# Swapping the two engines that issue loads and stores in a transfer-bound channel shuffle

## The chip, the cores and the metric

The kernel runs on one core of one Trainium2 chip. SyncE, ScalarE and VectorE are three of its engines, each with its own list of instructions. An engine that issues a transfer only hands it over (0.3 to 0.6 us in these traces); the core's 16 DMA engines then move the bytes, and the transfer has landed when all of them have arrived. The metric is the device time of one execution in microseconds (us), lower is better; a profile is a separate look at one execution, whose span is about 1.8 us shorter than its timed value. A run that is more than 1.5% above the fastest run of its own kernel counts as slow and is left out of ratios; where that happened it is said.

## The reference

A channel shuffle in float32: within every pixel, 256 channels seen as 8 groups of 32 are transposed to 32 by 8. No value changes.

```python
batch, h, w, c = 16, 64, 64, 256          # groups = 8
x = x.reshape(batch, h, w, groups, c // groups)
x = x.transpose(0, 1, 2, 4, 3)
return x.reshape(batch, h, w, c)
```

That is 67.11 MB in and 67.11 MB out.

## The kernel before

The pixels are cut into 16 tiles. `_SIZES` counts pixels per partition, so a tile of 38 is 128 rows of 38 x 256 floats = 38,912 contiguous bytes each, both in memory and on chip. Three input buffers, two output buffers. One engine, SyncE, issues all loads; VectorE transposes with one strided copy per tile; ScalarE issues all stores and does nothing else.

```python
_SIZES = [4, 8, 16] + [38] * 12 + [28]
_IN_BUFS = 3
_OUT_BUFS = 2
...
    for q in _SIZES:
        in_tile = in_pool.tile([P, biggest * c], F32, name="in_tile")
        nc.sync.dma_start(out=in_tile[:, : q * c], in_=rows(x_flat, first, q))      # line 47
        out_tile = out_pool.tile([P, biggest * c], F32, name="out_tile")
        nc.vector.tensor_copy(                                                      # line 49
            out=out_tile[:, : q * c].rearrange("p (i j g) -> p i j g", j=CPG, g=G),
            in_=in_tile[:, : q * c].rearrange("p (i g j) -> p i j g", g=G, j=CPG),
        )
        nc.scalar.dma_start(out=rows(out_flat, first, q), in_=out_tile[:, : q * c])  # line 53
        first += P * q
```

## Time and profile before

| | before |
|---|---|
| time, median of 3 | 316.71 us (316.44 to 317.62) |
| span of the profile | 314.7 us |
| VectorE busy | 119.2 us, 38% |
| share of the 16 DMA engines taken by the two queues | 49.8% + 49.4% |
| rate in the steady part | 433 GB/s |

The prediction below shows the lines behind this table. One more view of the kernel before is needed later: the timeline of the copies (start, duration, operation; in brackets the idle time of VectorE before it and what ended it).

```profile
20.36 3.90 DVE L49 COPY out_tile<-in_tile 128x4096 f32<-128x4096 f32 x1 [11.75 <-DMA out_dram<-out_tile]
34.50 8.75 DVE L49 COPY out_tile<-in_tile 128x9728 f32<-128x9728 f32 x1 [10.24 <-DMA out_dram<-out_tile]
51.03 8.75 DVE L49 COPY out_tile<-in_tile 128x9728 f32<-128x9728 f32 x1 [7.78 <-DMA out_dram<-out_tile]
74.00 8.80 DVE L49 COPY out_tile<-in_tile 128x9728 f32<-128x9728 f32 x1 [14.22 <-DMA out_dram<-out_tile]
```

Each of these copies waits for the store two tiles earlier, so their distances are the times of single stores: 14.1, 16.5 and 23.0 us, for stores whose rows have 8, 16 and 38 KB. Each store gives 128/16 = 8 rows to each DMA engine. At 433/16 = 27 GB/s per engine a row takes 0.30, 0.61 and 1.44 us. If every store row must let one 38 KB load row (1.44 us) go first, 8 turns make 8 x (1.44 + 0.30) = 13.9, 8 x (1.44 + 0.61) = 16.4 and 8 x (1.44 + 1.44) = 23.0 us. All three fit: an engine takes turns between the two queues by rows, and the length of a row does not count.

The distances alone would also fit turns of several rows at a time. The page's list of queues (packets, MB, share of the 16 engines; q1 carries the loads, q10 the stores), asked for 109.15 to 110.58 us and for 110.58 to 112.01 us, settles that:

```profile
q10 hardware_dynamic: 13, 0.51, 81.8%
q1 hardware_dynamic: 3, 0.12, 18.9%
...
q1 hardware_dynamic: 13, 0.51, 81.8%
q10 hardware_dynamic: 3, 0.12, 18.9%
```

In the time of one row, 13 store rows and 3 load rows start on the 16 engines; in the next it is the other way round, and so on in the two windows after these. An engine takes one row from each queue in turn.

### The profile page before, as it was taken

The numbers are of one execution on the slowest core, as the hardware profiler recorded it, in microseconds if no ns is written. First come the engines' busy times: TensorE is split into PE (matmuls) and PEld (weight loads), VectorE is DVE, ScalarE is ACT, GpSimd is POOL, SyncE is SP. The second block draws the span as 40 slices with busy tenths as digits, with TensorE's granted clock in tenths as the row PEclk, the third lists the DMA queues.
The fourth block names the chain that finished last, engine by engine and source line by source line (L and its number), as shares of the span: only waits on it lengthen the run. The fifth ranks groups of instructions, "written<-read, shape, count | busy, mean of one in ns | idle before, by whom it ended". The sixth has DMA issues, their size and how long they took to land.

```text
span 314.7 us, 133 instructions
## 1 busy us (share of the span) xinstructions
DVE 119.2 (38%) x16; POOL 0.2 (0%) x4
## 2 busy tenths in 40 slices
DVE  3040645505506407407308209109109019046620
POOL 0000000000000000000000000000000000000000
DMA  8999999999999999999999999999999999999997
GB/s 308 452 398 454 413 419 466 396 475 396 455 415 445 425 430 440 425 445 415 455 396 470 401 465 406 460 411 460 411 460 411 460 411 455 428 395 454 455 418 306
DMA packets 4608, 134.22 MB, mean 427 GB/s; under 512 B 512, under 2 KB 512, under 8 KB 768
## 3 DMA queue, kind: packets, MB, share of 16 engines
q1 hardware_dynamic: 2304, 67.11, 49.8%
q10 hardware_dynamic: 2304, 67.11, 49.4%
HBM read 67.11 MB, written 67.11 MB: 427 GB/s over the span
## 4 chain that ended last, share of the span: by engine, by line
DMA 75%; DVE 20%; issue 0%; SPq 0%; DVEq 0%
DMA out_dram<-out_tile 74%; DVE out_tile L49 20%; DMA in_tile<-in_x_dram 2%; SPq L47 0%; DVEq L49 0%
## 5 line engine op out<-in xcount | busy, mean ns | idle before, releaser
L49 DVE COPY out_tile<-in_tile 128x9728 f32<-128x9728 f32 (+4 forms) x16 | 119.2, 7449 | 181.4 <-DMA out_dram<-out_tile 175.9
L71 POOL MEMSET const-bfloat16-1.0<- 128x1 bf16 x1 | 0.1, 102 | 0.0
L71 POOL MEMSET const-uint8-127<- 128x1 uint8 x1 | 0.1, 102 | 0.0
L71 POOL MEMSET const-float32-1.0<- 128x1 f32 x1 | 0.1, 99 | 0.0
L71 POOL MEMSET const-float32-0.0<- 128x1 f32 x1 | 0.1, 98 | 0.2 <-issue 0.2
## 6 DMA issues: line engine op xcount, KB each, us to landing
in_tile<-in_x_dram SPq DMA_DIRECT2D x12, 4864.0 KB, 46.8
out_dram<-out_tile ACTq DMA_DIRECT2D x12, 4864.0 KB, 37.0
in_tile<-in_x_dram SPq DMA_DIRECT2D x1, 3584.0 KB, 43.8
out_dram<-out_tile ACTq DMA_DIRECT2D x1, 3584.0 KB, 13.3
in_tile<-in_x_dram SPq DMA_DIRECT2D x1, 2048.0 KB, 11.0
out_dram<-out_tile ACTq DMA_DIRECT2D x1, 2048.0 KB, 26.7
in_tile<-in_x_dram SPq DMA_DIRECT2D x1, 1024.0 KB, 5.4
out_dram<-out_tile ACTq DMA_DIRECT2D x1, 1024.0 KB, 25.8
```

What stands on the lines that cost most here:

```text
L49: nc.vector.tensor_copy(out=out_tile[:, : q * c].rearrange("p (i j g) -> p i j g", j=CPG, g=G), in_=in_tile[:, : q * c].rearrange("p (i g ...
L71: nc = _bacc.Bacc("TRN2", target_bir_lowering=False, num_devices=1)
```

## The change

The intent is to see whether it matters which engine issues which direction: the loads move to ScalarE and the stores to SyncE. Nothing else changes; the waits and the order of each list are the same.

```diff
-        nc.sync.dma_start(out=in_tile[:, : q * c], in_=rows(x_flat, first, q))
+        nc.scalar.dma_start(out=in_tile[:, : q * c], in_=rows(x_flat, first, q))
...
-        nc.scalar.dma_start(out=rows(out_flat, first, q), in_=out_tile[:, : q * c])
+        nc.sync.dma_start(out=rows(out_flat, first, q), in_=out_tile[:, : q * c])
```

## The prediction

> **What bounds the kernel now.** I read the page of the profile first: the busy table, the 40 slices and the queues.
>
> ```profile
> DVE 119.2 (38%) x16; POOL 0.2 (0%) x4
> ...
> DMA  8999999999999999999999999999999999999997
> GB/s 308 452 398 454 413 419 466 396 475 396 455 415 445 425 430 440 425 445 415 455 396 470 401 465 406 460 411 460 411 460 411 460 411 455 428 395 454 455 418 306
> ...
> q1 hardware_dynamic: 2304, 67.11, 49.8%
> q10 hardware_dynamic: 2304, 67.11, 49.4%
> HBM read 67.11 MB, written 67.11 MB: 427 GB/s over the span
> ```
>
> The only compute engine, VectorE, is busy 38% of the span. The 16 DMA engines are busy in every slice, with only the first and last below nine tenths. The two queues carry the same bytes and packets and fill 49.8% + 49.4% = 99.2% of what 16 engines have. So the transfers are the bound, and the GB/s row only wobbles because a slice catches more or fewer packet ends.
>
> Next I cut the span at the period of the copies (23 us, from the starts of the copies in the timeline) and at its two ends. The columns are the stretch, its length, VectorE and GpSimd busy time, clock, share of the DMA engines and GB/s.
>
> ```profile
> 152.00:175.00 23.00, 8.79 (x2) 0.00 (x0) 1.00 1.00 433
> 175.00:198.00 23.00, 8.85 (x2) 0.00 (x0) 1.00 1.00 433
> ...
> 1.50:1.70 0.20, 0.00 (x0) 0.00 (x0) 1.00 0.00 0
> 1.70:2.00 0.30, 0.00 (x0) 0.00 (x0) 1.00 1.13 205
> ...
> 312.00:313.00 1.00, 0.00 (x0) 0.00 (x0) 1.00 0.53 229
> 313.00:313.50 0.50, 0.00 (x0) 0.00 (x0) 1.00 0.01 0
> ```
>
> In the steady state the engines are full at 433 GB/s. Nothing moves before 1.7 us or after about 313 us. The ledger of the span is therefore: 134.22 MB / 433 GB/s = 310.0 us of transfer at full rate, 1.7 us of head, 1.7 us of tail (314.7 - 313.0), and 314.7 - 310.0 - 3.4 = 1.3 us of lost transfer while filling and draining. The timed run of the profiled execution is 316.46 us for a span of 314.7, so 1.8 us lies outside the span.
>
> Last come the waits, with engine, line, releaser, total us, times and longest.
>
> ```profile
> DVE out_tile L49 <- DMA out_dram<-out_tile: 175.9, 14, 14.6
> DVE out_tile L49 <- DMA in_tile<-in_x_dram: 5.5, 2, 4.1
> ...
> SPq L47 <- DVE out_tile L49: 224.4, 13, 22.2
> ```
>
> VectorE waits for an output buffer to be stored, 14 times; it waits for input only for the first two tiles. SyncE waits for a copy to free an input buffer. These waits say that everything stands behind the full transfer engines; none of them leaves an engine empty.
>
> **What the Trainium skill says.** "DMA: Bandwidth & Descriptors", section "Issuing engines are not separate DMA queues", says that DMAs from the scalar, sync or GpSimd engine all run on the same 16 DMA engines and interleave, so that the issuer only matters for the time of issuing. The trace agrees as far as it can: the two queues' shares add up to the one pool of 16. The same page, "SWDGE vs HWDGE vs iDMA", says a DMA issued from ACT is of the hardware kind just as one from SP; both queues are listed above as hardware_dynamic with 2304 packets each. The same page, "Queues, rings and completion order", says that each DMA engine goes round-robin between the queue rows, a whole packet at a time. That can be tested, because the first stores are small and meet large loads:
>
> ```profile
> in_tile<-in_x_dram SPq DMA_DIRECT2D x12, 4864.0 KB, 46.8
> out_dram<-out_tile ACTq DMA_DIRECT2D x12, 4864.0 KB, 37.0
> ...
> in_tile<-in_x_dram SPq DMA_DIRECT2D x1, 512.0 KB, 3.3
> out_dram<-out_tile ACTq DMA_DIRECT2D x1, 512.0 KB, 15.1
> ```
>
> The 512 KB store has 128 rows of 4 KB, 8 on each engine (128/16). One engine moves 433/16 = 27 GB/s, so a 4 KB packet is 0.15 us and a 38 KB row of a large load (9728 floats, 38912 bytes) is 1.44 us. If each store packet waits for one load packet, the store takes 8 x (1.44 + 0.15) = 12.7 us plus some 2 us of latency, that is 14.7; shown is 15.1. So the turns go one for one, and with equal packets each queue has half. "Perfetto Trace Analysis", section "Roofline", puts the ceiling of a single core at its 16 DMA engines, about 435 GB/s; 433 in the stretches above agrees, and leaves no room for a faster kernel with the same bytes.
>
> **The change part by part.** Nothing is added or removed. The two compiled programs compared instruction by instruction are equal on VectorE, GpSimd and TensorE; on ScalarE and SyncE the 16 loads and 16 stores change places, in the same order, with the same shapes and the same waits. Buffers stay at three and two. The cost is thus only in issuing:
>
> - First load, on the path: nothing can move before it. SyncE issues it at 0.73 us; its later load issues have a median of 328 ns, ScalarE's of 362 ns. So plus 0.03 us, perhaps a little more if ScalarE leaves the start barrier later.
> - The 15 other loads: 15 x 0.034 = 0.5 us in all, but each load is issued about a whole tile before it is needed. A load is issued when the copy three tiles earlier ends; its own copy starts 3 x 23 - 8.8 = 60 us later, and it lands after 46.8 us, so 13 us are spare. Hidden, 0.
> - The 16 stores: each gets about 0.03 us shorter on SyncE, and the engines have the rest of another transfer to move meanwhile. The last store is issued at 300.6 us, while the one before it, issued at 288.1, is still in flight. Hidden, 0.
> - The end: SyncE waits for the last stores at line 85 whichever engine issued them; issuing the stores first delays it by nothing, as its list is then empty. 0.
> - The sum is +0.03 us of 316.7, a hundredth of a per cent, below the spread of the three runs (316.44 to 317.62).
>
> **The rivals.**
>
> First, the turns might not be fair: one row (q1 or q10) may be favoured, and the swap would give the favour to the other direction. For it speaks only that the two directions have different landing times, 46.8 against 37.0 us; but that difference comes from how many transfers are queued behind one another, and the 15.1 us above says one for one. If stores were favoured, loads would come later, and the 13 us spare (6 us for the last load: VectorE is still waiting 5.95 us for a store before the last copy) would take it. Only a shift beyond that empties the engines; a period could then lose at most a few us, some 1% to 3%.
>
> Second, issuing on ScalarE could be a serial bottleneck: a load's issue and its semaphore waits sit on one in-order queue. Against it: one load per 23 us at 0.36 us of issue. Even 1 us of delay per load would be hidden by the 13 us. Worth at most 0.3 us, at the start.
>
> Third, a gain: SyncE's shorter issue for the stores, which are what VectorE waits for, could shorten the 175.9 us of waits. But these waits are transfer time of full engines; 0.03 us earlier into a queue with work before it changes nothing. A gain of 2% would need a span of some 308.4 us, or 305.0 without head and tail: 134.22 MB / 305.0 us = 440 GB/s, above any long stretch of the trace.
>
> **Range and chances.** 316.7 us, the median before plus 0.03. The range is the spread of the runs before, opened by about 0.4 us downwards for another draw and kept above: 316.0 to 317.6. Two per cent either way is 6.3 us; faster is excluded by the rate, slower needs the unfair turns. So 0.01, 0.98, 0.01.
>
> **What would show it right or wrong.** Right: 433 GB/s and a share of 1.00 in the 23 us stretches, the queues' shares swapped but adding to 99%, VectorE waiting some 176 us for stores, first bytes at about 1.75 us, the 512 KB store again near 15 us. Wrong: a head longer by over 0.3 us (ScalarE starts late); a stretch with a DMA share below 0.95, or VectorE waiting for loads in mid-kernel (unfair turns); landings of the 512 KB store much off 15 us.

## The result, and the profile after

The changed kernel takes 316.47 us (median of 6 runs, 316.39 to 317.35), the kernel before in the same rounds 316.63 us (316.44 to 317.62). The ratio is 0.9994 with a 95% interval of 0.9977 to 1.0012: the same. Ratios here are the mean time of one kernel's fast runs over the mean of the other's in the same rounds, so they are not quite the ratio of the medians.

From the page after its two queues (packets, MB, share), and then from the list of waits the largest (engine, line, what it waited for, total us, times, longest):

```profile
q10 hardware_dynamic: 2304, 67.11, 50.0%
q1 hardware_dynamic: 2304, 67.11, 49.3%
```

```profile
DVE out_tile L49 <- DMA out_dram<-out_tile: 176.2, 14, 15.0
```

The two queues have changed places in the list and are still full together (99.3%). VectorE waits for stores 176.2 us where it waited 175.9. The issue table after (operation, count, KB each, median us to landing) for the large tiles:

```profile
in_tile<-in_x_dram ACTq DMA_DIRECT2D x12, 4864.0 KB, 47.1
out_dram<-out_tile SPq DMA_DIRECT2D x12, 4864.0 KB, 37.0
```

Landing times stayed with the direction (46.8 and 37.0 before) and did not follow the engine. The first copy starts at 4.11 us, before at 4.09.

The profiled execution after happens to be its slowest run: a span of 315.6 us against 314.7. Two stretches of it (columns as in the prediction):

```profile
175.00:198.00 23.00, 8.84 (x2) 0.00 (x0) 1.00 1.00 433
...
221.00:244.00 23.00, 8.20 (x2) 0.00 (x0) 1.00 0.98 418
```

In the second stretch a pair of copies (212.50 and 236.07 us) is 23.57 us apart instead of 22.97; an earlier pair (50.88 and 74.64 us) lost 0.8 us. These are single hiccups of the transfers. Four of the six runs after have 316.4 to 316.5 us and so none of that size, and the kernel before has runs of 317.2 and 317.6, so they say nothing about the change.

### The profile page after: what moved, and what is told of

Its sections match the earlier page's. It is cut to its first block, busy times and chain, and to the rows that moved or that the text cites. A ratio compares the mean times of both kernels' runs of the same rounds, so it can differ in the third digit from the quotient of the medians.

```text
span 315.6 us, 133 instructions
## 1 busy us (share of the span) xinstructions
DVE 119.8 (38%) x16; POOL 0.2 (0%) x4
## 3 DMA queue, kind: packets, MB, share of 16 engines
q10 hardware_dynamic: 2304, 67.11, 50.0%
q1 hardware_dynamic: 2304, 67.11, 49.3%
## 4 chain that ended last, share of the span: by engine, by line
DMA 75%; DVE 20%; issue 0%; ACTq 0%; DVEq 0%
DMA out_dram<-out_tile 74%; DVE out_tile L49 20%; DMA in_tile<-in_x_dram 2%; ACTq L47 0%; DVEq L49 0%
## 5 line engine op out<-in xcount | busy, mean ns | idle before, releaser
L49 DVE COPY out_tile<-in_tile 128x9728 f32<-128x9728 f32 (+4 forms) x16 | 119.8, 7489 | 181.6 <-DMA out_dram<-out_tile 176.2
## 6 DMA issues: line engine op xcount, KB each, us to landing
in_tile<-in_x_dram ACTq DMA_DIRECT2D x12, 4864.0 KB, 47.1
```

The costliest lines, as they stand in the source:

```text
L49: nc.vector.tensor_copy(out=out_tile[:, : q * c].rearrange("p (i j g) -> p i j g", j=CPG, g=G), in_=in_tile[:, : q * c].rearrange("p (i g ...
```

## The experiments

The theory: 16 full DMA engines set the time, and the issuing engine, SyncE or ScalarE, matters neither for the issue cost (hidden) nor for the share of the engines (turns are per row). The rivals of the prediction were unfair turns, a slower issuer that delays loads, and earlier stores that help. A delay can be made large enough to see, and turns can be made unequal on purpose.

### Loads issued late (e3, e9)

The changed kernel, with eight ScalarE copies into the buffer ahead of a load:

```diff
+        if i >= 5:                       # e9: if 8 <= i < 15
+            for k in range(8):
+                nc.scalar.copy(out=in_tile[:, :2400], in_=scratch[:, :])
         nc.scalar.dma_start(out=in_tile[:, : q * c], in_=rows(x_flat, first, q))
```

> The changed kernel, with eight ScalarE copies of 2400 columns into the input tile ahead of every load from the sixth on: each of these loads is issued some 17 us later (an estimate), far more than the 0.03 us by which the two engines differ. Theory: a load's 47 us to landing are mostly time behind the load before it, so a load issued 17 us later lands in about 30 us; nothing waits; 316.3 to 317.8 us, VectorE waits for loads in mid-kernel under 3 us in total. Rival (the spare is only the 13 us between landing and use, as the prediction has it): 4 us per round of three buffers, 3 P = 17.5 + 47 + 8.8, so P = 24.4 instead of 23 us, times 11 tiles: about 331 us, with VectorE waiting for loads.

Measured: 320.88 us (319.30 to 322.15; ratio 1.0132). Neither number: far from the rival's 331, but not the same either. The windows of the profile (stretch, length, VectorE, ScalarE, GpSimd busy, clock, DMA share, GB/s) show where:

```profile
35.00:60.00 25.00, 18.32 (x2) 24.22 (x12) 0.00 (x0) 1.00 0.92 376
...
129.00:152.00 23.00, 9.19 (x1) 17.61 (x9) 0.00 (x0) 1.00 1.00 433
```

From 35 to 60 us the engines were partly empty: the first large tiles come only 14 and 16.5 us apart, ScalarE needs 17.6 us per delayed load, and it fell behind (busy 24.22 of 25 us). In the steady part the engines are full at 433 GB/s despite the delay. So the delay was moved to the steady part alone:

> As the late loads before, but the delay of some 17.5 us stands only ahead of seven loads in the steady part (the ninth to the fifteenth tile), so that ScalarE has no backlog from the early tiles, which come 14 and 16.5 us apart. Theory: a late load is hidden in the steady part: 316.3 to 317.8 us, and the loads it concerns land about 17 us sooner after issue. Rival (the 1.3 per cent of the earlier run came from the late issue itself): 318.5 us or more.

Measured: 317.01 us against 316.78, ratio 1.0003 (0.9986 to 1.0020). The issue table of this run:

```profile
in_tile<-in_x_dram ACTq DMA_DIRECT2D x12, 4864.0 KB, 28.5
```

The load is issued some 17.6 us later and lands 18.6 us sooner after issue than the 47.1 us of the changed kernel. Most of a load's landing time is time behind the load before it. A delay some 500 times the 0.034 us by which the two issuers differ is hidden in the steady part.

### Stores issued late (e5)

The kernel before, with two in-place ScalarE copies ahead of ten stores:

```diff
+        if 5 <= i < 15:
+            for k in range(2):
+                nc.scalar.copy(out=out_tile[:, :2400], in_=out_tile[:, :2400])
         nc.scalar.dma_start(out=rows(out_flat, first, q), in_=out_tile[:, : q * c])
```

> The kernel before (stores on ScalarE), with two ScalarE copies in place on 2400 columns of the output tile ahead of ten of the stores: each of these is issued some 4.4 us later (an estimate). Theory: a store issued that much later still finds the store before it in flight (it has 14 us to go), so it lands in about 33 us instead of 37; the time stays: 316.3 to 317.8 us. Rival (VectorE waits 176 us for stores, so when a store is issued sets the pace): 2 P = 8.8 + 4.4 + 37, P = 25.1 instead of 23 us, times 10: about 337 us.

Measured: 317.19 us against 316.52, ratio 1.0015 (0.9999 to 1.0031): the same.

```profile
out_dram<-out_tile ACTq DMA_DIRECT2D x12, 4864.0 KB, 32.5
```

The stores land 4.5 us sooner after issue (32.5 for 37.0): the delay of 4.38 us is paid out of the time in the queue. VectorE's 176 us of waiting for stores is waiting for full engines; when a store is issued does not set its length, within these 4.4 us.

### A late first load (e4)

```diff
+        if i == 0:
+            for k in range(4):
+                nc.scalar.copy(out=in_tile[:, :1024], in_=ones[:, :])
```

> The changed kernel, with four small ScalarE copies (and a fill of their source on VectorE) ahead of the first load alone. Theory: before the first load nothing else can keep the DMA engines busy, so here a delay counts in full: the span grows by as much as the issue of the first load moves from 0.72 us, expected 5 to 8 us, so 321.5 to 324.5 us. Rival (delays at issue are hidden wherever they stand): 316.5 us.

Measured: 322.46 us, ratio 1.0181 (1.0163 to 1.0199), 5.8 us more by the medians. In the timeline the loads of this run begin at

```profile
6.32 59.71 ACTq L54 DMA_DIRECT2D in_tile<-in_x_dram  x8
```

instead of 0.72 us: 5.6 us later, and the time follows in full. Of the places that the runs delayed, only this one puts the few hundredths of a microsecond of issue cost on the path. The last store was delayed by no run: e5 leaves it out. (In the changed kernel the few hundredths were not even there: the first load is issued at 0.72 us by ScalarE, at 0.73 by SyncE before.)

### Unequal turns (e1, e2), their control (e10) and the other queue (e11)

A gap of 64 bytes in the middle of a tile's rows makes the transfer send each row as two packets of half the length (3968 packets in the cut queue instead of 2304). With one packet per turn, a direction that is cut gets a smaller share while the other is not.

```diff
-            nc.scalar.dma_start(out=in_tile[:, : q * c], in_=rows(x_flat, first, q))
+            nc.scalar.dma_start(                     # e1: loads of 38 and 28 pixels
+                out=halves(in_tile, q),
+                in_=rows(x_flat, first, q).rearrange("p (k f) -> p k f", k=2),
+            )
```

> The changed kernel, but the rows of the large loads go as two pieces of 19 KB (a gap in the input tile), those of the stores whole. Theory (each DMA engine takes one packet per turn from each queue, and all work is hidden behind 16 full engines): the stores get the larger share while both queues have work, so the early stores land sooner; the copies of the fourth and fifth tile, 14.1 and 16.5 us after the one before them now (8 turns of 1.44 + 0.31 and 1.44 + 0.61 us), come about 8 x (0.72 + 0.31) = 8.3 and 8 x (0.72 + 0.61) = 10.7 us apart. The time stays at 316.5 us, plus at most 1 us for the doubled number of load packets: 316.3 to 317.8. Rival (shares do not follow packets, or an unequal share empties the engines): the early copies keep their distances of 14 and 16.5 us, or the time rises by 1 to 3 per cent (320 to 326).

Measured: 327.95 us (323.74, 326.25, 329.65, 330.77). The ratio of 1.0264 uses only the two faster runs, because the other two are over 1.5% above the fastest; the mean of all four gives 1.035. The theory was right about the shares and wrong about the time. From the issue table of e1:

```profile
in_tile<-in_x_dram ACTq DMA_DIRECT2D x12, 4864.0 KB, 57.3
out_dram<-out_tile SPq DMA_DIRECT2D x12, 4864.0 KB, 22.1
```

Loads land after 57.3 us instead of 47.1, stores after 22.1 instead of 37.0. Now loads are what VectorE waits for (180.3 us). The expected distances of 8.3 and 10.7 us can't be read from the copies any more, because these wait for loads. The stores themselves show them: the first three are issued at 5.08, 8.49 and 20.54 us and land 11.5, 17.3 and 16.1 us later, about 9.2 and 10.8 us apart instead of 14.1 and 16.5.

> The changed kernel, but the rows of the large stores go as two pieces of 19 KB, those of the loads whole: stores now get one third of an engine's time while loads have work. Theory: loads can only run three buffers ahead, then the stores have the engines for themselves; the engines stay full, landing times of stores get longer or uneven, the time stays: 316.3 to 317.8 us. Rival (turns unfair against the stores, which VectorE waits for, cost 1 to 3 per cent): 320 to 326 us, with stretches below 0.95 of the DMA engines.

Measured: 322.78 us, ratio 1.0200 (1.0173 to 1.0227). The rival's range again. The engines are not empty, however; a window of e2:

```profile
198.00:221.00 23.00, 11.90 (x2) 0.00 (x0) 1.00 0.99 407
```

A share of 0.99 at 407 GB/s means that packets took longer. The trace also keeps a record of every packet (queue, size, start, duration). Those of e2 say which: the cut store rows stay at 0.72 to 0.79 us, but some of the whole load rows, usually 1.44 us, take up to 2.8 us, in bursts (165 to 185, 215 to 225 and 260 to 275 us). After 60 us this adds up to 3.9 us per engine (before: 0.1), of the 6.3 us by which the span is longer. Is it the cut itself? In the control both directions are cut:

> The control for the two runs with cut rows: rows of large loads and of large stores both go in two pieces, so the turns are equal again and only the number of packets is doubled. Theory (unequal turns made the loss): only the cost of the packets stays, an estimate of 1 to 2 us, so 317.3 to 318.7 us, VectorE waiting for stores again and copies 23 us apart. Rival (the cut itself, the gap in the tile or the smaller packets, made it): 322 us or more.

Measured: 317.30 us, ratio 1.0014 (0.9999 to 1.0029). So neither the gap nor the doubled packets cost anything visible (the 1 to 2 us expected for them was a guess); rows unequal between the two sides did. One part of the expectation failed in an instructive way, as the waits and the timeline of e10 show:

```profile
DVE out_tile L63 <- DMA in_tile<-in_x_dram: 173.6, 13, 14.6
```

```profile
137.95 8.50 DVE L63 COPY out_tile<-in_tile 128x9728 f32<-128x9728 f32 x1 [14.54 <-DMA in_tile<-in_x_dram]
161.00 8.51 DVE L63 COPY out_tile<-in_tile 128x9728 f32<-128x9728 f32 x1 [14.55 <-DMA in_tile<-in_x_dram]
```

VectorE waits 174 us for loads and none for stores of large tiles, the opposite of the kernel before, with the same 23 us between copies and the same time. So the direction that a compute engine is seen waiting for does not tell the bound. My reading is that it shows which direction got ahead at the start, where the short rows of the first stores meet load rows of half the length; no run tests that.

Last, the cut loads in the kernel before, so that the longer queue belongs to SyncE:

> The kernel before (loads on SyncE, stores on ScalarE) with the rows of the large loads in two pieces. Theory (a queue's share follows from its packets and not from which engine's queue it is): the same as the same cut in the changed kernel, 324 to 331 us, with VectorE waiting some 180 us for loads. Rival (one of the two queues is favoured): a time or a split of waits clearly apart from that run, such as stores waited for, or 320 us or below.

Measured: 327.74 us (325.36 to 328.85; ratio 1.0333), against 327.95 us of e1 (on another chip; the kernel before took 316.78 and 316.52 us beside them). The spread of e1 is 7 us, so the times alone only exclude a favour of some 2%. The pattern is sharper. The same copy in e1 and in e11:

```profile
80.06 8.52 DVE L63 COPY out_tile<-in_tile 128x9728 f32<-128x9728 f32 x1 [23.01 <-DMA in_tile<-in_x_dram]
```

```profile
80.12 8.49 DVE L63 COPY out_tile<-in_tile 128x9728 f32<-128x9728 f32 x1 [23.02 <-DMA in_tile<-in_x_dram]
```

The first seven copies agree within 0.1 us, though loads and stores have changed queues. Shares follow packets, not the queue or its engine. A part of the loss in e1 and e11 lies at the end. In e11 the last load comes too late to have a store beside its copy:

```profile
308.99 6.30 DVE L63 COPY out_tile<-in_tile 128x7168 f32<-128x7168 f32 x1 [12.08 <-DMA in_tile<-in_x_dram]
```

```profile
310.00:315.00 5.00, 5.00 (x1) 0.00 (x0) 1.00 0.07 31
```

During the last copy the engines stand at a share of 0.07. In e1 the last copy (from 302.8 us) still has a store beside it, at shares of 0.90 and 0.98; there the engines are emptier just before, at 0.81 and 0.76 from 290 to 300 us. In the kernel before this copy runs from 294.0 us beside a store that lasts to about 305.

Cutting the spans at 280 us shows how the losses divide. The kernel before moves 430 GB/s up to there and 402 from there to its end; e2 moves 420 and 404, e1 424 and 366, e11 426 and 326. So all of the 6.3 us that e2 loses by its span are lost before 280 us, at a share of 0.99; of e1's 7.3 us about half; of e11's 11.3 us less than 3, and the rest at the end, with engines partly empty.

### Each direction alone (e8)

To explain the longer packets of e2, a new theory was that loads are slower when all 16 engines read at once. This run gives a wrong result: all loads first, then all stores.

> A wrong result on purpose: first all 16 loads, with no stores beside them, then (after one copy) all 16 stores from one tile. It measures each direction by itself. New theory, after the runs with unequal turns were 2 per cent slower with full engines: packets of loads get slower when all 16 engines read at once, so the loads alone move at 405 to 425 GB/s at a share of the DMA engines near 1.00, and the stores alone at 433. Rival (reading alone is as fast as mixed): both at 433 GB/s, 155 us each.

Measured in one look (321.84 us, a single run whose state is unknown; only the windows matter):

```profile
20.00:50.00 30.00, 0.00 (x0) 0.00 (x0) 1.00 1.01 436
...
210.00:240.00 30.00, 0.00 (x0) 0.00 (x0) 1.00 1.01 436
```

The first window has only loads, the second only stores, both at 436 GB/s; the four 30 us windows of loads have 422 to 436, the four of stores 419 to 436. The new theory fell: in the packet records no large load row of this run takes more than 1.45 us. Why load rows take longer in parts of e2 stays open.

### One list for both directions (e6, e7)

Both directions issued by SyncE; for e6 the difference from the changed kernel is one line:

```diff
-        nc.scalar.dma_start(out=in_tile[:, : q * c], in_=rows(x_flat, first, q))
+        nc.sync.dma_start(out=in_tile[:, : q * c], in_=rows(x_flat, first, q))
```

> Loads and stores all issued by SyncE, in the program order of the kernel. Theory: the engine that issues does not matter, but what stands in one list does: a load is now issued only after the store ahead of it, which waits for its copy, so nothing is loaded ahead. Per large tile 23 us of transfers and then a copy of 8.8 us with empty engines: about 32 us, times 13: some 415 to 440 us. Rival (all issue lists feed the same 16 engines, so one list is as good as two): 317 us.

Measured: 474.57 us, ratio 1.498 (1.495 to 1.500). The timeline of e6:

```profile
217.88 8.85 DVE L49 COPY out_tile<-in_tile 128x9728 f32<-128x9728 f32 x1 [25.53 <-DMA in_tile<-in_x_dram]
226.75 0.33 SPq L53 DMA_DIRECT2D out_dram<-out_tile  x1
227.13 0.43 SPq L47 DMA_DIRECT2D in_tile<-in_x_dram  x1
252.27 8.78 DVE L49 COPY out_tile<-in_tile 128x9728 f32<-128x9728 f32 x1 [25.54 <-DMA in_tile<-in_x_dram]
```

The next load is issued only at 227.13, after the store that waited for the copy, though a buffer was free earlier. The period is 34.4 us = 8.8 of copy + 25.5 of transfers. Direction and mechanism were right; the estimate of 32 us left out some 2.5 us beside the 23 us of pure transfer, each time in the open: 0.4 us until the load is issued, the rest until it has landed.

In e7 the loads stand two tiles earlier in the same list (`load(i + 2)` ahead of the copy and the store of tile `i`):

> Loads and stores all issued by SyncE again, but each load is placed two tiles earlier in the list, ahead of the store that it would have waited behind. Theory: the engines are full again, and neither a second queue nor the turns between queues are needed: 316 to 318 us; the first store of 512 KB, now behind two small loads in one queue, lands in 6 to 8 us instead of 15. Rival (two queues are needed for full engines, one for each direction): above 325 us.

Measured: 320.86 us, ratio 1.0133 (1.0106 to 1.0159); the 512 KB store landed after 9.1 us. Between the two expectations. The order in the list accounts for nearly all of the 158 us that e6 lost, but 4 us remain: windows from 60 to 129 us have 433 GB/s at a share of 1.00, the early one has

```profile
5.00:35.00 30.00, 12.64 (x4) 0.00 (x0) 1.00 1.02 418
```

which is 1 us short, and some later ones have 425 to 431. What causes these was not looked into. No version here beats the two kernels.

## Why the prediction was right

- **The sum.** It put the cost at +0.03 us and the time at 316.7; measured 316.47 with an interval of the ratio of -0.2% to +0.1%. That is as far as it can be tested.
- **The first load.** Predicted on the path, +0.03 us or more. It is on the path (e4: 5.6 us of delay, 5.8 us of time), and cost nothing to be seen: issue at 0.72 instead of 0.73 us.
- **The other loads, hidden.** Issue did get longer as said (median 366 ns on ScalarE, 328 on SyncE before). The conclusion holds (e9), but the reason given, 13 us of spare, was too small: a delay of 17.6 us in the steady part was absorbed, because landing time shrinks with it. In the early tiles ScalarE fell behind with such a delay, and e3 lost time there.
- **The stores, hidden.** Right for the ten stores that e5 delayed: 4.38 us late cost nothing clear of noise. The last store is argued only.
- **Turns one for one.** Right, but the working with the 512 KB store was partly lucky. It assumed a 38 KB load row in each of 8 turns and some 2 us of latency (the 512 KB load takes 3.3 us, 1.2 of them for its bytes at 433 GB/s); the 2 MB load with 16 KB rows was still in the queue until 12.6 us (issued at 1.6, 11.0 to land). In the packet records of the kernel before the rows of that store run from 9.4 to 18.5 us. So of the 15.1 us, 4.2 passed before the first row, 9.1 with the 8 turns (not 12.7) and 1.8 until landing: two errors cancelled, and why the first row starts so late was not looked into. In e1, where large load rows are half as long, that store landed 3.5 us sooner (11.5 for 15.0), which is about 5 rows x 0.72 us, not 8. The copy distances of 14.1, 16.5 and 23.0 us and the packets per row time are the clean evidence, and the distances are the same after the change (14.1 and 16.5; the third was hit by a hiccup).
- **The rivals.** The first was sized at 1% to 3%: turns made unequal on purpose did cost 2.0% to 3.3% (e2, e1, e11; 3.5% for e1 by all its runs), and the last copy without enough spare, which the prediction had named, is visible in e11. It did not happen here, because the share does not depend on the queue's owner (e11 against e1). The second is answered by e9. For the third, e5 shows that later stores cost nothing, and the result shows no gain from earlier ones; the prediction's 440 GB/s "above any long stretch" is loose, as 267 to 288 us has 442, but 60 us from 40 us on have 437.
- **The signs of being wrong.** Two of them would have misled. A stretch with a share below 0.95 does not appear in the windows (12 to 30 us long) between 5 and 300 us of e2, which lost 2.0%. VectorE waiting for loads in mid-kernel does appear in e10, with equal turns and no loss.

## What to carry to other kernels

When full DMA engines set the time, ask of an issuing change the three things that cost time here: does it delay the first transfer, does it put a wait ahead of a transfer that could have gone (e6: 50%), and does it alter the length of rows on one side (2% to 3%). Whether SyncE or ScalarE issues is none of them (ScalarE had nothing else to do here; GpSimd was not tried). Do not read a large wait for one direction as that direction being the bound: two kernels with equal times waited 174 us for loads and 176 us for stores.

## What the Trainium skill lacked or had wrong

- "DMA: Bandwidth & Descriptors", section "Queues, rings and completion order", says that the engines go round-robin at packets, but not what follows for the shares: here a row counts as one turn at any length up to 38,912 bytes, so single stores took 14.1, 16.5 and 23.0 us for rows of 8, 16 and 38 KB beside the same loads, and halving the load rows moved the landing times from 47.1 and 37.0 us to 57.3 and 22.1 us. It gives 9 to 17 descriptors as typical of a packet; the profile counts 2304 packets per queue, which is 16 transfers x 128 rows and 256 small ones (512 packets under 512 bytes in the two queues), one packet per row, and within one row time 13 and 3 rows of the queues start, then 3 and 13.
- No page says that unequal turns cost time while the bytes stay the same: ratios 1.0200, 1.0264 and 1.0333 with one side cut, 1.0014 with both cut.
- "DMA: Bandwidth & Descriptors", section "Rules for kernel authors", says that spreading transfers over several issuing engines only saves issue time. Two lists also keep a load from standing behind a store's wait: 474.57 us with one list against 316.63 with two, and 320.86 with one list in another order.
